# Score matmuls over 128 rows with zero-padded k pieces, and bisection on fp32 scores, in a hybrid attention layer

## Chip, core and metric

The kernel runs on one core of one Trainium2 chip. The metric is the device time of one execution in microseconds (us). Its engines are TensorE (PE in the rows; PEld is its weight load), VectorE (DVE), ScalarE (ACT), GpSimd (POOL) and SyncE (SP), which issues most DMAs.

## The reference

One encoder layer over x of 1024 frames by 1024 features, fp32. One input projection feeds three groups of heads; their outputs go through an output projection, a layer norm, a SwiGLU network of width 2816 and a second layer norm. Cut to what the change touches:

```
h = x @ w_in
# differential attention: 4 heads, two score maps each, 64 features, blocks of 128 queries
logits = einsum('bthmd,bshmd->bhmts', q, k) * scale + alibi bias, masked by chunks of 64
p = softmax(logits); attn = p[:, :, 0] - lam * p[:, :, 1]; out_b = rms_norm(attn @ v)
# sparse attention: 4 heads of 64 features; of each query's allowed keys the 256 best by an index score
score = sum over 8 index heads of w * relu(q_i @ k_i)
_, sel = lax.top_k(score, 256)
out_c = softmax(q @ k[sel] * scale + bias) @ v[sel]
```

## The kernel before

Matrix products keep fp32 accuracy by splitting an operand into a high part in fp32r (rounded) and a low part, the rest. A projection is three matmuls for each piece (`mm3`, L180 to L182): high by high, high by low, low by high.

**Scores.** A head's q and k hold 64 features for each of two score maps m. `q_stacks` puts q's high part on 64 partitions and its low part on the other 64 of one tile. `k_stacks` (L629 on) copies k's high part to both halves of `kh[m]` (a copy by ScalarE and a DMA from half to half), so that one matmul over 128 rows gives q's high plus low part by k's high part (L659, weights 128 x 128). The missing product, q's high part by k's low part, is a second matmul into the same PSUM piece (L660); k's low parts of both maps share one tile, `kl`, 64 partitions each, and the matmul works on those 64 rows alone. `softmax` does this for pieces of 256 to 512 columns, and VectorE then takes each piece out of PSUM with bias and running minimum (L664). `diff_unit` makes one block of 128 queries of a differential head (names b0 to b3), `dsa_pair` two sparse heads (c0, c1). There are 8 blocks for each of 6 pairs of maps.

**Selection.** The index scores of query blocks 2 to 7 lie in `sc_all` in fp32. The 256th largest of a row is found by bisection over the 32 bits of its key: a step counts how many scores reach a candidate. ScalarE does the counting for blocks 5 to 7, VectorE for blocks 2 to 4 (`DVE_B`; 640, 512 and 384 columns). VectorE first copies the upper 16 bits of its scores to a packed tile (`upper_halves`, L493), and counts over those for bits 31 to 16 (L497). Then `lower_halves` (L505 to L520) counts scores above the found upper half, and replaces each score by its lower 16 bits where the upper half is equal and by zero where it isn't; 16 steps more count over those (`bisect_low`, L529 to L532).

**Order.** Lists in the file say in which order attention units are made (`UNITS`), how many projection pieces go between them (`FILLS`), and how many bisection steps of either engine (`STEPS_A`, `STEPS_D`). A scheduler then interleaves the instructions at build time; each engine runs its own list in order. Tiles of 4 KB for each partition come from a ring `st` of 11 buffers: all of q, k, the packed scores, later weights. Transposed probabilities use `at`, 3 buffers. GpSimd splits weights of projections (L170, L158) and makes two small operations of each differential unit: `sn` (L692) and the power in `rsqrt` (`rs`, L198), for which VectorE waits (L704). The SwiGLU network comes after all attention, from about 650 us on.

Of the kernel before, what the change touches and what calls it, by code (L numbers as in the profile page):

```python
# [9 lines left out]
F32 = mybir.dt.float32  # L10
# [88 lines left out]
def trunk(  # L99
# [22 lines left out]
        return t if len(shape) == 2 else t.rearrange("p (a b) -> p a b", a=shape[1])  # L122

    def st(name, shape=(P, 1024), dt=F32R):
        return tl("st", 11, name, shape, dt)

    def pp(name, shape=(P, 1024), dt=F32):
        return tl("p", 5, name, shape, dt)
# [7 lines left out]
    def small(name, w=1, dt=F32, bufs=5):  # L136
        return pool.tile([P, w], dt, tag=f"s_{name}", bufs=bufs, name=name)
# [13 lines left out]
    def f(ap):  # L151
        return ap.bitcast(F32)
# [322 lines left out]
    junk, junk_a = junk2[:, 0], junk2[:, 1]  # L475
    zero = pool.tile([P, len(SEL_BLOCKS)], I32, name="zero")
    V.memset(zero, 0)
    flips, half = {}, {}

    def as_float(dst, k, e):  # L480
        t = small(f"bt_{e}", nbl[e], I32, 2)
        V.tensor_scalar(t, k, 31, 0x7FFFFFFF, op0=OP.arith_shift_right, op1=OP.bitwise_and)
        V.scalar_tensor_tensor(dst, k, -1, t, op0=OP.bitwise_xor, op1=OP.bitwise_xor)

    def upper_halves():
        free, t = 0, None
        for i in sorted(DVE_B, key=lambda i: (i == 2, -i)):
            n = P * (i + 1)
            if free < n:
                t, free = st(f"half{i}", (P, 2048), BF16), 2048  # L490
            half[i] = t[:, 2048 - free:2048 - free + n]
            free -= n
            V.tensor_copy(half[i], SC[i].bitcast(BF16)[:, 1::2])  # L493

    def count_half(th, cnt, dt):
        for j, i in enumerate(DVE_B):
            V.tensor_scalar(junk[:, 0:P * (i + 1)], half[i].bitcast(dt), th[:, j:j + 1], None,  # L497
                            op0=OP.is_ge, op1=OP.add, accum_out=cnt[:, j:j + 1])

    low = {}  # L500

    def lower_halves():
        key, nb = keys["d"], nbl["d"]
        top = small("top", nb, I32, 1)
        V.scalar_tensor_tensor(top, key, 0, flips["d"], op0=OP.bitwise_or, op1=OP.bitwise_xor)  # L505
        sg = small("sgn", nb, F32, 1)
        V.tensor_copy(sg, key)
        V.tensor_scalar(sg, sg, 0.0, None, op0=OP.is_ge)
        off = small("off", nb, F32, 1)
        V.tensor_scalar(off, sg, 65535.0, None, op0=OP.mult)  # L510
        V.tensor_scalar(sg, sg, -2.0, 1.0, op0=OP.mult, op1=OP.add)
        need = small("need_d", nb, F32, 1)
        for j, i in enumerate(DVE_B):
            n = P * (i + 1)
            t = f(top)[:, j:j + 1]
            V.tensor_scalar(junk[:, 0:n], half[i], t, None, op0=OP.is_gt, op1=OP.add, accum_out=need[:, j:j + 1])
            V.tensor_scalar(junk[:, 0:n].bitcast(U16), SC[i].bitcast(U16)[:, 0::2], sg[:, j:j + 1], off[:, j:j + 1],
                            op0=OP.mult, op1=OP.add)
            V.scalar_tensor_tensor(half[i].bitcast(U16), half[i], t, junk[:, 0:n].bitcast(U16), op0=OP.is_equal, op1=OP.mult)
        V.tensor_scalar(need, need, -1.0, TOPK - 0.25, op0=OP.mult, op1=OP.add)  # L520
        lk = small("low", nb, F32, 1)
        V.memset(lk, 0.0)
        low["need"], low["key"] = need, lk

    def bisect_low(b):
        nb, lk = nbl["d"], low["key"]
        cand = small("cand", nb, F32, 2)
        cnt = small("cnt_d", nb, F32, 2)
        V.tensor_scalar(cand, lk, float(1 << b), None, op0=OP.add)  # L529
        count_half(cand, cnt, U16)  # L530
        V.tensor_tensor(cnt, cnt, low["need"], OP.is_ge)
        V.scalar_tensor_tensor(lk, cnt, float(1 << b), lk, op0=OP.mult, op1=OP.add)  # L532
        if b == 0:
            li = small("lowi", nb, I32, 1)
            V.tensor_copy(li, lk)
            V.tensor_tensor(keys["d"], keys["d"], li, OP.bitwise_or)

    def bisect(b, e):
        if e == "d" and b == 31:
            upper_halves()  # L540
        if e == "d" and b < 16:
            if b == 15:
                lower_halves()
            bisect_low(b)
            return
        key = keys[e]
        cnt = small(f"cnt_{e}", nbl[e], F32, 2)
        fl = small(f"fl_{e}", nbl[e], I32, 2)
        if b == 31:
            cf = zero[:, 0:nbl[e]]  # L550
        else:
            cf = small(f"cf_{e}", nbl[e], I32, 2)
            V.scalar_tensor_tensor(cf, key, 1 << b, flips[e], op0=OP.bitwise_or, op1=OP.bitwise_xor)  # L553
        if e == "d":
            count_half(f(cf), cnt, BF16)
            V.tensor_scalar(fl, cnt, TOPK - 0.25, None, op0=OP.is_ge)
        else:
            for j, i in enumerate(ACT_B):
                A.activation(junk_a[:, 0:P * (i + 1)], SC[i], AF.Sign, bias=f(cf)[:, j:j + 1], accum_out=cnt[:, j:j + 1])  # L559
            V.tensor_tensor(fl, cnt, lim, OP.is_ge)  # L560
        V.scalar_tensor_tensor(key, fl, b, key, op0=OP.logical_shift_left, op1=OP.bitwise_or)
        if b == 31:
            m = pool.tile([P, nbl[e]], I32, name=f"flip_{e}")
            V.tensor_scalar(m, key, 31, 0x7FFFFFFF, op0=OP.arith_shift_right, op1=OP.bitwise_and)
            V.tensor_scalar(m, m, -1 if e == "d" else 0x7FFFFFFF, -65536 if e == "d" else -1, op0=OP.bitwise_xor, op1=OP.bitwise_and)
            flips[e] = m

    def settle():
# [60 lines left out]
    def k_stacks(col, name, rh, rl):  # L629
        wh, wl = wload(win[:, :, col:col + P], name, [P, KC, P], GP)  # L630
        yield
        kh = [st(f"{name}_h{m}") for m in range(2)]
        kl = st(f"{name}_l")
        rh += kh
        rl += [kl[0:64], kl[64:128]]
        for half in range(2):
            ps = proj_t(wh, wl, P, half)
            sl = slice(half * 512, half * 512 + 512)
            for m in range(2):
                a = slice(64 * m, 64 * m + 64)  # L640
                b = slice(64 - 64 * m, 128 - 64 * m)
                A.activation(kh[m][a, sl], ps[a], AF.Copy)
                sub(V, kl[a, sl], ps[a], f(kh[m][a, sl]))
                nc.sync.dma_start(f(kh[m][b, sl]), f(kh[m][a, sl]))
            yield

# [6 lines left out]
    def softmax(i, m, q, kh, kl, bias, slope, p):  # L653
        n = P * (i + 1)
        nm = None
        sm = small("sm")
        for o, w in pieces(n):
            ps = ps_qk("psq")
            nc.tensor.matmul(ps[:, 0:w], q[:, i * P:(i + 1) * P], kh[:, o:o + w], start=True, stop=False)  # L659
            nc.tensor.matmul(ps[:, 0:w], q[64 * m:64 * m + 64, i * P:(i + 1) * P], kl[:, o:o + w], start=False, stop=True)  # L660
            w = min(w, n - o)
            prev = BIG if nm is None else nm
            nm = small(f"nm{o}")
            V.tensor_tensor_reduce(out=p[:, o:o + w], in0=ps[:, 0:w], in1=bias[:, o:o + w], scale=-slope, scalar=prev,  # L664
                                   op0=OP.add, op1=OP.min, accum_out=nm)
        A.activation(p[:, 0:n], p[:, 0:n], AF.Exp, bias=nm, scale=-1.0, accum_out=sm)  # L666
        return p, sm

    def prio(n):
        return tc.high_priority(n)  # L670

    def attend(i, a, vsl, ps):
        nk = i + 1
        for j0 in range(0, nk, 4):
            jn = min(4, nk - j0)
            pt = ps_tr("psa")
            for j in range(jn):
                nc.tensor.transpose(pt[:, j * P:(j + 1) * P], a[:, (j0 + j) * P:(j0 + j + 1) * P], ident)
            at = tl("at", 3, "at", (P, 512))
            A.activation(at[:, 0:jn * P], pt[:, 0:jn * P], AF.Copy)  # L680
            for j in range(jn):
                nc.tensor.matmul(ps, at[:, j * P:(j + 1) * P], vsl(j0 + j), start=(j0 + j == 0), stop=(j0 + j == nk - 1))  # L682
# [96 lines left out]
    def dsa_pair(c, i):  # L779
# [10 lines left out]
        for j0 in range(0, nk, 4):  # L790
            jn = min(4, nk - j0)
            at = []
            for m in range(2):
                pt = ps_tr("psa")
                for j in range(jn):
                    nc.tensor.transpose(pt[:, j * P:(j + 1) * P], pr[m][:, (j0 + j) * P:(j0 + j + 1) * P], ident)
                at.append(tl("at", 3, "at", (P, 512)))
                copy(at[m][:, 0:jn * P], pt[:, 0:jn * P], "av"[m])
            for j in range(jn):
                for m in range(2):  # L800
                    hs = slice(64 * m, 64 * m + 64)
                    nc.tensor.matmul(ps[hs], vc[c][:, j0 + j, hs], at[m][:, j * P:(j + 1) * P],
                                     start=(j0 + j == 0), stop=(j0 + j == nk - 1))
# [171 lines left out]
            sub(V, l, r[k], f(h))  # L975
        return T

    def w4(name, tag="st", bufs=11):
        return tl(tag, bufs, name, (P, KC, P), F32R)

    def hidden(c):
# [172 lines left out]
```

## Time and profile before

| what | value |
|---|---|
| median of 3 runs | 1423.05 us (1419.74 to 1425.28) |
| the profiled execution | 1420.1 us |
| its span, first to last instruction | 1418.3 us |
| mean granted TensorE clock | 0.955 of full |
| TensorE busy | 94% of the span |
| VectorE, ScalarE, GpSimd busy | 65%, 39%, 22% |

Shares are means over stages with different limits, and a busy TensorE is one that has a matmul in its pipe, whether or not the next could have started sooner. How fast matmuls follow each other is read from the differences of their starts in the timeline.

### The profile page before, as it was taken

The page shows a single profiled execution, that of the slowest core. Times are in us where ns is not written, and L with a number is a line of the kernel's source. Part 1 is how long each engine was busy: PE and PEld are TensorE (multiplying, and loading weights), DVE is VectorE, ACT ScalarE, POOL GpSimd, SP SyncE. Part 2 cuts the span into 40 slices and gives each one's busy share as a digit, 9 for nine tenths or more (in the row PEclk, how much of TensorE's full clock was granted, in tenths as well). Part 3 has the DMA queues.
Part 4 walks back from the last instruction along what each step waited for, and adds up shares of the span by engine and source line. Part 5 has one row for each costly group of instructions (what it writes and reads, how often), then busy time and mean ns, then how long its engine had stood idle before and what let it go on. Part 6 is the DMA issues. An engine that isn't in the chain of part 4 may idle for free.

```text
span 1418.3 us, 17526 instructions
## 1 busy us (share of the span) xinstructions
PE 1329.7 (94%) x6444; PEld 1065.8 (75%) x6444; DVE 927.0 (65%) x1821; ACT 557.6 (39%) x1033; POOL 318.3 (22%) x250
## 2 busy tenths in 40 slices
PE   7568987988999999899999999999999999999997
PEld 6457665676787886557788888888888888888886
DVE  5137899797657968444859776676667655348325
ACT  4145565666785534243313322222222233213310
POOL 1203221103132144400215333233333210000003
PEclk9779998899999999889999999999999999999999
DMA  6221111101111111315402222222222248427501
GB/s 192 76 74 59 49 29 43 36 9 38 51 40 41 50 34 49 96 51 182 149 33 91 86 74 90 89 79 85 90 77 75 87 182 336 149 89 269 206 0 60
DMA packets 107685, 127.46 MB, mean 90 GB/s; under 512 B 8144, under 2 KB 80720, under 8 KB 107600
## 3 DMA queue, kind: packets, MB, share of 16 engines
q1 hardware_dynamic: 106448, 122.15, 26.4%
q10 hardware_dynamic: 1152, 4.19, 0.8%
q8 instruction: 51, 0.84, 0.3%
q14 instruction: 34, 0.28, 0.1%
HBM read 97.49 MB, written 25.69 MB: 87 GB/s over the span
## 4 chain that ended last, share of the span: by engine, by line
PE 51%; DVE 1%; DMA 0%; issue 0%; ACT 0%; DVEq 0%; ACTq 0%; SPq 0%
PE p L181 9%; PE p L182 9%; PE p L180 9%; PE psd L180 6%; PE psd L182 6%; PE psd L181 6%; PE psz L182 1%; PE psz L180 1%; PE psz L181 1%; PE pg L180 1%; PE pu L182 1%; PE pu L180 1%; PE pg L182 1%; PE pg L181 1%; PE pu L181 1%; PE pst L208 0%
## 5 line engine op out<-in xcount | busy, mean ns | idle before, releaser
L559 ACT ACTIVATE junk<-sc_all,cf_a 128x768 bf16<-128x768 f32 (+2 forms) x93 | 96.7, 1039 | 35.9 <-DVE cf_a L553 14.1
L182 PE MATMUL psn<-hi_n,xTl 128*128 128x256 f32 x320 | 99.0, 309 | 0.0
L180 PE MATMUL psn<-hi_n,xTh 128*128 128x256 f32 x320 | 97.5, 305 | 0.9 <-DVE nm L664 0.9
L181 PE MATMUL psn<-lo_n,xTh 128*128 128x256 f32 x320 | 96.8, 302 | 0.0
L666 ACT ACTIVATE pt<-pt,nm 128x128 f32<-128x128 f32 (+7 forms) x96 | 74.0, 772 | 49.4 <-DVE nm L664 47.0
L198 POOL TENSOR_TENSOR lrs<-rv,mhalf 128x1 f32<-128x1 f32 x16 | 20.6, 1286 | 307.5 <-DVE rv L195 307.5
L1017 POOL TENSOR_TENSOR s<-raw_u 128x512 f32<-128x512 f32 x20 | 27.9, 1396 | 242.4 <-DMA raw_u<-in_w_gu_dram 206.9
L180 PEld LDWEIGHTS psn<-hi_n,xTh 128*128 128x128 f32 x320 | 66.2, 207 | 4.2 <-issue 2.0
L182 PEld LDWEIGHTS psn<-hi_n,xTl 128*128 128x128 f32 x320 | 66.2, 207 | 4.2 <-issue 3.0
L181 PEld LDWEIGHTS psn<-lo_n,xTh 128*128 128x128 f32 x320 | 65.8, 206 | 3.2 <-issue 1.6
L180 PE MATMUL p<-x1Th,gh 128*128 128x512 f32 x160 | 62.2, 389 | 0.0
L181 PE MATMUL p<-x1Tl,gh 128*128 128x512 f32 x160 | 62.2, 389 | 0.0
L182 PE MATMUL p<-x1Th,gl 128*128 128x512 f32 x160 | 62.2, 389 | 0.0
L365 PE MATMUL psi<-kst,qst 128*128 128x512 f32 (+1 forms) x80 | 29.0, 398 | 32.5 <-DMA qst<-qd 21.3
L372 DVE SCALAR_TENSOR_TENSOR sc_all<-rl,iw,sc_all 128x384 f32<-128x384 f32 (+5 forms) x42 | 41.4, 1046 | 27.5 <-ACT rl L367 27.4
L1043 DVE TENSOR_TENSOR th<-p,tp 128x512 f32<-128x512 f32 x20 | 13.8, 692 | 69.1 <-DMA hd<-th 57.6
L1059 ACT ACTIVATE sg<-tp 128x512 f32<-128x512 f32 x20 | 12.7, 634 | 105.6 <-DVE tp L1058 105.6
L664 DVE CUSTOM_DVE_ANT_0 pt<-psq,dist 128x512 f32<-128x512 f32 (+3 forms) x72 | 38.8, 546 | 22.0 <-PE psq L660 21.7
L198 POOL TENSOR_TENSOR rs<-rv,mhalf 128x1 f32<-128x1 f32 x32 | 19.1, 597 | 134.5 <-DVE rv L197 79.4
L1040 ACT ACTIVATE tp<-p 128x512 f32<-128x512 f32 x20 | 12.0, 600 | 93.6 <-DVE th L1065 80.4
L367 ACT ACTIVATE rl<-psi 128x512 f32<-128x512 f32 (+1 forms) x80 | 35.4, 562 | 23.7 <-PE psi L365 21.1
L682 PEld LDWEIGHTS pso<-vb,at 128*128 128x128 f32 x288 | 39.1, 206 | 7.0 <-DVE ob L705 2.4
(679 smaller groups left out, 4168.1 us busy)
## 6 DMA issues: line engine op xcount, KB each, us to landing
raw_g<-in_w_gu_dram SPq DMA_DIRECT2D x22, 512.0 KB
raw_u<-in_w_gu_dram SPq DMA_DIRECT2D x22, 512.0 KB
hd<-th SPq DMA_DIRECT2D x22, 512.0 KB
raw_n<-in_w_in_dram SPq DMA_DIRECT2D x10, 512.0 KB
x<-in_x_dram SPq DMA_DIRECT2D x8, 512.0 KB
raw_wo<-in_w_out_dram SPq DMA_DIRECT2D x8, 512.0 KB
mx<-mixd SPq DMA_DIRECT2D x8, 512.0 KB
y<-x1d SPq DMA_DIRECT2D x8, 512.0 KB
```

Of the source, the lines that this page charges most:

```text
L180: nc.tensor.matmul(ps, lh, rh, start=first, stop=False)
L181: nc.tensor.matmul(ps, lh, rl, start=False, stop=False)
L182: nc.tensor.matmul(ps, ll, rh, start=False, stop=last)
L198: GP.tensor_tensor(o, t, mhalf[:, 0:w], OP.pow)
L365: nc.tensor.matmul(ps[:, 0:w], qst[h][:, (i - 2) * P:(i - 1) * P], kst[:, o:o + w], start=True, stop=True)
L367: A.activation(r[:, o:o + w], ps[:, 0:w], AF.Relu)
L372: V.scalar_tensor_tensor(SC[i], r[:, 0:n], wcol, SC[i], op0=OP.mult, op1=OP.add)
L559: A.activation(junk_a[:, 0:P * (i + 1)], SC[i], AF.Sign, bias=f(cf)[:, j:j + 1], accum_out=cnt[:, j:j + 1])
L664: V.tensor_tensor_reduce(out=p[:, o:o + w], in0=ps[:, 0:w], in1=bias[:, o:o + w], scale=-slope, scalar=prev, op0=OP.add, op1=OP.min, accum ...
L666: A.activation(p[:, 0:n], p[:, 0:n], AF.Exp, bias=nm, scale=-1.0, accum_out=sm)
L682: nc.tensor.matmul(ps, at[:, j * P:(j + 1) * P], vsl(j0 + j), start=(j0 + j == 0), stop=(j0 + j == nk - 1))
L1017: GP.tensor_tensor(a[:, 0:4], u[:, 0:4], u[:, 4:8], OP.add)
```

## The change

`k_stacks` takes a tile of its own for each map's low part: 64 partitions hold it, and GpSimd sets the other 64 to zero. The second score matmul takes all 128 rows of q and of that tile. Where the low part meets q's high part the product is as before, and the zero rows add nothing. The ring `st` gets a twelfth buffer. The bisection of blocks 2 to 4 counts over the fp32 scores in `sc_all` for all 32 bits; the packed tile and its two preparations go. The transposed probabilities go in turn to four parts of one fixed tile, `ats`, in place of three buffers.

```diff
     def st(name, shape=(P, 1024), dt=F32R):
-        return tl("st", 11, name, shape, dt)
+        return tl("st", 12, name, shape, dt)
...
-    def upper_halves():
...
-            V.tensor_copy(half[i], SC[i].bitcast(BF16)[:, 1::2])
-
-    def count_half(th, cnt, dt):
-        for j, i in enumerate(DVE_B):
-            V.tensor_scalar(junk[:, 0:P * (i + 1)], half[i].bitcast(dt), th[:, j:j + 1], None,
-                            op0=OP.is_ge, op1=OP.add, accum_out=cnt[:, j:j + 1])
...
-    def lower_halves():
...
-    def bisect_low(b):
...
     def bisect(b, e):
-        if e == "d" and b == 31:
-            upper_halves()
-        if e == "d" and b < 16:
-            if b == 15:
-                lower_halves()
-            bisect_low(b)
-            return
...
         if e == "d":
-            count_half(f(cf), cnt, BF16)
+            for j, i in enumerate(DVE_B):
+                V.tensor_scalar(junk[:, 0:P * (i + 1)], SC[i], f(cf)[:, j:j + 1], None,
+                                op0=OP.is_ge, op1=OP.add, accum_out=cnt[:, j:j + 1])
...
         kh = [st(f"{name}_h{m}") for m in range(2)]
-        kl = st(f"{name}_l")
+        kl = [st(f"{name}_l{m}") for m in range(2)]
         rh += kh
-        rl += [kl[0:64], kl[64:128]]
+        rl += kl
+        for m in range(2):
+            GP.memset(f(kl[m][64 - 64 * m:128 - 64 * m]), 0.0)
...
-                sub(V, kl[a, sl], ps[a], f(kh[m][a, sl]))
+                sub(V, kl[m][a, sl], ps[a], f(kh[m][a, sl]))
...
-            nc.tensor.matmul(ps[:, 0:w], q[64 * m:64 * m + 64, i * P:(i + 1) * P], kl[:, o:o + w], start=False, stop=True)
+            nc.tensor.matmul(ps[:, 0:w], q[:, i * P:(i + 1) * P], kl[:, o:o + w], start=False, stop=True)
...
+    ats = pool.tile([P, 4, 512], F32, name="ats")
+    turn = iter(range(1 << 20))
+
+    def next_at():
+        return ats[:, next(turn) % 4]
...
-            at = tl("at", 3, "at", (P, 512))
+            at = next_at()
...
-    def w4(name, tag="st", bufs=11):
+    def w4(name, tag="st", bufs=12):
```

The line numbers of the changed kernel are about 53 lower behind the removed functions: L606 and L607 are its two score matmuls, L496 its count.

TensorE, where the scores of a block of head b2 stand between pieces of the projection of b3's q (psp) and products of probabilities and values (pso); before:

```order
L682 MATMUL pso<-vb_2357,at 128x128 x3
L182 MATMUL psp<-xTh_71,lo_b3q 128x512
L659 MATMUL psq<-b2k_h_2098,b2q_1982 128x512
L180 MATMUL psp<-xTh_71,hi_b3q 128x512
L660 MATMUL psq<-b2k_l,b2q_1982 128x512
L181 MATMUL psp<-xTl_73,hi_b3q 128x512
L182 MATMUL psp<-xTh_71,lo_b3q 128x512
L659 MATMUL psq<-b2k_h_2098,b2q_1982 128x256
L682 MATMUL pso<-vb_2357,at 128x128 x4
L180 MATMUL psp<-xTh_71,hi_b3q 128x512
L660 MATMUL psq<-b2k_l,b2q_1982 128x256
L181 MATMUL psp<-xTl_73,hi_b3q 128x512
```

and now:

```order
L180 MATMUL psp<-xTh_71,hi_b3q 128x512
L181 MATMUL psp<-xTl_73,hi_b3q 128x512
L606 MATMUL psq<-b2k_h_2087,b2q_1972 128x512
L182 MATMUL psp<-xTh_71,lo_b3q 128x512
L607 MATMUL psq<-b2k_l_2089,b2q_1972 128x512
L180 MATMUL psp<-xTh_71,hi_b3q 128x512
L181 MATMUL psp<-xTl_73,hi_b3q 128x512
L606 MATMUL psq<-b2k_h_2087,b2q_1972 128x256
L182 MATMUL psp<-xTh_71,lo_b3q 128x512
L607 MATMUL psq<-b2k_l_2089,b2q_1972 128x256
L180 MATMUL psp<-xTh_71,hi_b3q 128x512
```

The two score matmuls of a piece still stand one matmul of the projection apart; what stands between them and around them has shifted by a few rows.

VectorE, where the bisection of blocks 2 to 4 (names ending in d, `half`, `junk`) passes from bit 16 to bit 15; before:

```order
L497 TENSOR_SCALAR junk_490,cnt_d<-half_1245,cf_d 128x640
L693 RECIPROCAL r_2279<-sm 128x1
L556 TENSOR_SCALAR fl_d<-cnt_d 128x3
L694 TENSOR_TENSOR r_2279<-r_2279,sn 128x1
L561 SCALAR_TENSOR_TENSOR key_d<-fl_d,key_d 128x3
L695 SCALAR_TENSOR_TENSOR pt<-pt,r_2279 128x512
L505 SCALAR_TENSOR_TENSOR top<-key_d,flip_d 128x3
L507 CAST sgn<-key_d 128x3
L516 TENSOR_SCALAR junk_490,need_d<-half_1245,top 128x384
L508 TENSOR_SCALAR sgn<-sgn 128x3
L510 TENSOR_SCALAR off<-sgn 128x3
L511 TENSOR_SCALAR sgn<-sgn 128x3
```

and now, at the same bit:

```order
L496 TENSOR_SCALAR junk_490,cnt_d<-sc_all,cf_d 128x512
L493 SCALAR_TENSOR_TENSOR cf_a<-key_a,flip_a 128x3
L496 TENSOR_SCALAR junk_490,cnt_d<-sc_all,cf_d 128x640
L498 TENSOR_SCALAR fl_d<-cnt_d 128x3
L503 SCALAR_TENSOR_TENSOR key_d<-fl_d,key_d 128x3
L493 SCALAR_TENSOR_TENSOR cf_d<-key_d,flip_d 128x3
L496 TENSOR_SCALAR junk_490,cnt_d<-sc_all,cf_d 128x384
L496 TENSOR_SCALAR junk_490,cnt_d<-sc_all,cf_d 128x512
L158 TENSOR_TENSOR b2k_l_2089<-psp,b2k_h_2087 64x512
L611 ISA pt,nm_2377<-psq,dist,nm_2372 128x256
L611 ISA nm_2377 128x1
L496 TENSOR_SCALAR junk_490,cnt_d<-sc_all,cf_d 128x640
```

Before, the preparation of the lower halves begins here; now the next count over `sc_all` follows at once.

GpSimd, after the splitting of head b2's q weights, among the small operations of the units of head b0; before:

```order
L158 TENSOR_TENSOR lo_b2q<-raw_b2q,hi_b2q 128x1024
L692 TENSOR_TENSOR sn<-sm,neglam 128x1
L198 TENSOR_TENSOR rs<-rv_1198,mhalf 128x1
L692 TENSOR_TENSOR sn<-sm,neglam 128x1
L198 TENSOR_TENSOR rs<-rv_1303,mhalf 128x1
L692 TENSOR_TENSOR sn<-sm,neglam 128x1 x2
L170 TENSOR_SCALAR hi_b2k<-raw_b2k 128x1024
L158 TENSOR_TENSOR lo_b2k<-raw_b2k,hi_b2k 128x1024
```

and now:

```order
L158 TENSOR_TENSOR lo_b2q<-raw_b2q,hi_b2q 128x1024
L645 TENSOR_TENSOR sn<-sm,neglam 128x1
L198 TENSOR_TENSOR rs<-rv_1201,mhalf 128x1
L645 TENSOR_TENSOR sn<-sm,neglam 128x1
L198 TENSOR_TENSOR rs<-rv_1301,mhalf 128x1
L645 TENSOR_TENSOR sn<-sm,neglam 128x1
L582 MEMSET b1k_l_1725 64x1024
L582 MEMSET b1k_l_1726 64x1024
L645 TENSOR_TENSOR sn<-sm,neglam 128x1
L170 TENSOR_SCALAR hi_b2k<-raw_b2k 128x1024
L158 TENSOR_TENSOR lo_b2k<-raw_b2k,hi_b2k 128x1024
```

The two memsets of head b1's low parts now stand in GpSimd's list between two `sn`. The other ten stand among its work too: b0's between two weight splits, b2's on either side of an `rs`.

## Rows read from the trace of the kernel before

**Rows 1.** The page, part 1: busy us of each engine, share of the span, instructions.
```profile
PE 1329.7 (94%) x6444; PEld 1065.8 (75%) x6444; DVE 927.0 (65%) x1821; ACT 557.6 (39%) x1033; POOL 318.3 (22%) x250
```

**Rows 2.** Source line L660: first and last of six rows, TensorE alone (144 matmuls).
```profile
L660 PE MATMUL psq<-b0k_l,b0q x24: 379/439/792, 147.7 to 185.5; 64*128 64x512 f32 x10, 64*128 64x256 f32 x8, 64*128 64x384 f32 x6
...
L660 PE MATMUL psq<-c1k_l,c1q x24: 275/498/792, 582.0 to 645.8; 64*128 64x512 f32 x10, 64*128 64x256 f32 x8, 64*128 64x384 f32 x6
```

**Rows 3.** Windows: busy us by engine in three stretches, granted clock, DMA share, GB/s.
```profile
147.00:350.00 203.00, 176.74 (x819) 131.84 (x818) 180.49 (x656) 127.56 (x296) 40.48 (x55) 0.89 0.12 32
350.00:650.00 300.00, 286.50 (x1623) 216.32 (x1621) 199.48 (x500) 159.15 (x347) 87.13 (x68) 0.93 0.18 52
650.00:1418.30 768.30, 759.97 (x3434) 626.05 (x3432) 475.40 (x558) 213.57 (x268) 166.50 (x108) 1.00 0.34 118
```

**Rows 4.** Waits from 147 to 650 us: total us, times, longest us.
```profile
DVE pt L664 <- PE psq L660: 37.6, 37, 5.8
...
PE psa L678 <- DVE pt L695: 15.0, 7, 3.9
...
DVE rs L704 <- POOL rs L198: 7.8, 14, 0.7
```

**Rows 5.** TensorE's timeline at 293 us: start us, us, instruction.
```profile
293.17 0.41 PE L182 MATMUL psn<-hi_n,xTl 128*128 128x256 f32 x1
293.38 0.38 PE L180 MATMUL psn<-hi_n,xTh 128*128 128x256 f32 x1
...
293.72 0.28 PE L182 MATMUL psn<-hi_n,xTl 128*128 128x256 f32 x1
293.84 0.28 PE L659 MATMUL psq<-b2k_h,b2q 128*128 128x256 f32 x1
294.05 0.38 PE L660 MATMUL psq<-b2k_l,b2q 64*128 64x256 f32 x1
294.36 0.38 PE L180 MATMUL psn<-hi_n,xTh 128*128 128x256 f32 x1
```

**Rows 6.** TensorE's timeline at 405 us.
```profile
405.33 0.40 PE L659 MATMUL psq<-b3k_h,b3q 128*128 128x512 f32 x1
405.56 0.28 PE L180 MATMUL psn<-hi_n,xTh 128*128 128x256 f32 x1
405.77 0.49 PE L660 MATMUL psq<-b3k_l,b3q 64*128 64x512 f32 x1
406.20 0.38 PE L181 MATMUL psn<-lo_n,xTh 128*128 128x256 f32 x1
```

**Rows 7.** Windows of source line L660 alone: TensorE and its weight load.
```profile
147.00:350.00 203.00, 30.02 (x63) 12.35 (x63) 0.89 0.12 32
```

**Rows 8.** Groups by form on VectorE, 147 to 460 us: busy us, mean ns, idle before.
```profile
L497 DVE TENSOR_SCALAR_CACHE_REDUCE junk<-half,cf_d 128x640 bf16<-128x640 bf16 x15 | 13.1, 877 | 0.2
...
L531 DVE TENSOR_TENSOR cnt_d<-cnt_d,need_d 128x3 f32<-128x3 f32 x16 | 5.6, 351 | 0.2
...
L556 DVE TENSOR_SCALAR fl_d<-cnt_d 128x3 int32<-128x3 f32 x16 | 3.7, 229 | 0.2
...
L606 DVE TENSOR_SCALAR_CACHE_REDUCE eq<-sc_all,thr_d 128x640 f32<-128x640 f32 x1 | 0.9, 872 | 0.0
```

**Rows 9.** Source lines L493, L516, L517, L519: duration ns min/median/max, starts.
```profile
L493 DVE COPY half<-sc_all x3: 360/411/475, 146.2 to 147.7; 128x640 bf16<-128x640 bf16 x1, 128x512 bf16<-128x512 bf16 x1, 128x384 bf16<-128x384 bf16 x1
...
L516 DVE TENSOR_SCALAR_CACHE_REDUCE junk<-half,top x3: 612/748/879, 244.9 to 249.4; 128x384 bf16<-128x384 bf16 x1, 128x512 bf16<-128x512 bf16 x1, 128x640 bf16<-128x640 bf16 x1
...
L517 DVE TENSOR_SCALAR junk<-sc_all,sgn,off x3: 479/547/600, 246.1 to 251.3; 128x384 uint16<-128x384 uint16 x1, 128x512 uint16<-128x512 uint16 x1, 128x640 uint16<-128x640 uint16 x1
...
L519 DVE SCALAR_TENSOR_TENSOR half<-half,top,junk x3: 621/752/877, 246.6 to 254.9; 128x384 uint16<-128x384 bf16 x1, 128x512 uint16<-128x512 bf16 x1, 128x640 uint16<-128x640 bf16 x1
```

**Rows 10.** Groups by form on GpSimd, whole span.
```profile
masks.py:197 POOL MEMSET ident<- 128x128 f32 x1 | 0.2, 204 | 0.3 <-POOLq L1141 0.3
```

**Rows 11.** GpSimd's timeline at 139 us, with the wait before.
```profile
138.63 1.06 POOL L170 TENSOR_SCALAR hi_b1k<-raw_b1k 128x1024 fp32r<-128x1024 f32 x1 [7.52 <-PE psp L181]
```

More of the change, by code (lines that the diff above doesn't have):

```diff
@@ L477, in trunk @@
     V.memset(zero, 0)
-    flips, half = {}, {}
+    flips = {}
     def as_float(dst, k, e):
@@ L483, in as_float @@
         V.scalar_tensor_tensor(dst, k, -1, t, op0=OP.bitwise_xor, op1=OP.bitwise_xor)
-    def upper_halves():
[L486 to L492, printed above, removed]
-            V.tensor_copy(half[i], SC[i].bitcast(BF16)[:, 1::2])
-    def count_half(th, cnt, dt):
-        for j, i in enumerate(DVE_B):
-            V.tensor_scalar(junk[:, 0:P * (i + 1)], half[i].bitcast(dt), th[:, j:j + 1], None,
-                            op0=OP.is_ge, op1=OP.add, accum_out=cnt[:, j:j + 1])
@@ L500, in trunk @@
-    low = {}
-    def lower_halves():
[L503 to L523, printed above, removed]
@@ L525, in bisect_low @@
-    def bisect_low(b):
[L526 to L536, printed above, removed]
@@ L564, in bisect @@
             V.tensor_scalar(m, key, 31, 0x7FFFFFFF, op0=OP.arith_shift_right, op1=OP.bitwise_and)
-            V.tensor_scalar(m, m, -1 if e == "d" else 0x7FFFFFFF, -65536 if e == "d" else -1, op0=OP.bitwise_xor, op1=OP.bitwise_and)
+            if e == "a":
+                V.tensor_scalar(m, m, 0x7FFFFFFF, None, op0=OP.bitwise_xor)
+            else:
+                V.tensor_scalar(m, m, -1, None, op0=OP.bitwise_xor)
             flips[e] = m
@@ L796, in dsa_pair @@
                     nc.tensor.transpose(pt[:, j * P:(j + 1) * P], pr[m][:, (j0 + j) * P:(j0 + j + 1) * P], ident)
-                at.append(tl("at", 3, "at", (P, 512)))
+                at.append(next_at())
                 copy(at[m][:, 0:jn * P], pt[:, 0:jn * P], "av"[m])
```

## Prediction

> **What bounds the kernel now.** I read the busy shares first: TensorE 94%, VectorE 65%, the others far below [rows 1]. A share is a mean over stages, so I then cut the span into windows at the first and the last of the second score matmuls, about 147 and 650 us [rows 2]. Behind 650 us TensorE is busy 760.0 of 768.3 us at full granted clock [rows 3]; no edit removes work there, so whatever is won ahead of 650 us should reach the end, as that stage merely starts sooner. All the rest is decided in the two windows before it. From 350 to 650 us TensorE is busy 286.5 of 300 us and VectorE 199.5: TensorE sets the pace. From 147 to 350 us TensorE is busy 176.7 of 203 us and VectorE 180.5: both are near their limit and take turns. In the table of waits [rows 4] the reader should see both directions: VectorE waited 37.6 us for the second score matmul, and TensorE's transposes waited 15.0 us for VectorE's probabilities. So in these windows time saved on either engine may count, and the question is how much of it.
>
> **The second score matmul.** The busy column hides its cost, so I take differences of starts. At 293 us an ordinary 256-column matmul over 128 rows is followed after 0.12 us (293.72 to 293.84). The same matmul ahead of the 64-row one takes 0.21 (293.84 to 294.05), and the 64-row one is followed after 0.31 (294.05 to 294.36) [rows 5]. Against 0.12 each that is 0.09 + 0.19 = 0.28 us lost around one matmul. At 405 us the ordinary 512-column step is 0.23 (405.33 to 405.56); the step into the 64-row matmul is 0.21 where 256 columns want 0.12, and the step out of it 0.43 where 512 want 0.23: 0.29 us [rows 6]. The zero-padded matmul has the shape of its neighbours, so I take their steps for it. The rows name 144 of them, 24 for each of six heads [rows 2]: 144 x 0.29 = 41.8 us of TensorE's time. By place, 63 lie from 147 to 350 us [rows 7], worth 18.3 us, and the other 81 behind it, worth 23.5 us. None of this shows as idle, since a 64-row matmul is recorded as 439 to 498 ns long in the medians [rows 2] and overlaps the next.
>
> From 350 to 650 us the bound is the whole 23.5 us below, and nothing above, where each step ended in front of another wait. TensorE isn't alone there, because transposes wait for probabilities and heads of the sparse part go through three engines in turn; I take three quarters, 17.6 us.
>
> **The bisection on VectorE.** A count over 640 packed 16-bit scores takes 877 ns; the same operation over 640 fp32 scores in the final selection takes 872 [rows 8]. So the 96 counts cost the same in both forms, and what goes is preparation. The three copies take 0.36, 0.41 and 0.48 us; the counts above, the low pieces and the masks take 2.24, 1.63 and 2.25 [rows 9]: together 7.4 us. Some nine operations on 128 x 3 numbers go with them, priced by the 229 ns of such an operation [rows 8] at no more than 2.1 us; I take 1.5. Each of the 16 lower steps compares by an operation of 351 ns where the upper steps compare by one of 229: 16 x 0.12 = 2.0 us. The sum is 10.9 us less on VectorE, all from 147 to 350 us and shortly behind.
>
> The Trainium skill, VectorE: DVE Perf Modes, section "The perf-mode tier table", says that a scalar operation on 16-bit data in SBUF runs at four elements a cycle and on fp32 at two. By its figures for 2048 elements (693 and 1227 ns) the fp32 counts would cost an estimated 0.26 ns an element more, 1536 x 32 x 0.26 = 12.8 us, and VectorE would gain nothing. The measured counts show no difference between the two types, so the measurement decides.
>
> **The window from 147 to 350 us.** If VectorE sets the pace throughout, the gain there is its 10.9 us; if TensorE does, it is 18.3. They alternate, and I take the middle, 14.6 us. The lower bound of the gain is nothing, when the waits of one for the other merely move.
>
> **GpSimd's memsets.** Twelve, 64 x 1024. The nearest row below is a memset of 128 x 128, 0.20 us [rows 10]; above, a weight split of 128 x 1024, 1.06 [rows 11]. I take 1.0, since the elements for each partition are those of the split: 12 us in all on an engine busy 22% [rows 1]. For head b0 the cover is a wait of 7.52 us just behind the split of b1's q [rows 11], and two memsets fit in. The others stand between `sn` and `rs`, and behind them VectorE waits already, 7.8 us in 14 times [rows 4]. If every pair of the other five held one up by its 2 us, that would be 10 us; they fall where GpSimd is idle four times out of five, so I take 1 us.
>
> **The rest.** The twelfth buffer replaces the one that packed scores held, while two heads at a time take one more each; a wait for it would be TensorE's or ScalarE's at a head's start. No row prices that beside the memsets' waits; I bound it by nothing and by their 10 us, and take nothing. The fourth buffer for transposed probabilities can only take away a wait, and costs nothing. The SwiGLU stage has one buffer more and TensorE never waits there long enough to notice: 8.3 us idle in 768 [rows 3].
>
> **Sum.** 17.6 + 14.6 - 1 = 31.2 us. From the profiled 1420.1 us that is 1388.9; the median of the three runs is 3 us above that execution, so I predict 1392 us.
>
> **The rivals.**
>
> *Half is absorbed.* VectorE keeps the pace up to 350 us and the chains between engines keep it behind, so that only VectorE's 10.9 us and a quarter of the 23.5 arrive: 17 us, and 11 with some of the memsets' 10. For it speaks VectorE's 180.5 of 203 us; against it, that VectorE itself waits 37.6 us for this matmul [rows 4]. 1406 us, from 1400 to 1412.
>
> *More than the steps.* The granted clock averages 0.89 and 0.93 in the two windows [rows 3]. A mean of two levels, 1.0 and 0.5, makes that (0.11 x 203 + 0.07 x 300) x 2 = 87 us at 1.2 GHz. There a 256-column step takes 0.21 us (293.17 to 293.38) against 0.12 [rows 5]. If TensorE, with fewer stalls, kept 2.4 GHz in a third of that, 29 x 0.43 = 12 us come on top, and with all 41.8 us of steps the time is 1371. For it speaks that in the last window, where TensorE never pauses, the clock is 1.00; against it, that TensorE still waits for VectorE.
>
> *The fp32 counts are slower after all*, by the 12.8 us above (the output is 16-bit, which the fp32 row isn't): then the first window gives at most a few us, and the time is about 1404. The two equal rows speak against it.
>
> *No change.* The steps only exposed waits that ended at the same time anyway, and the VectorE savings were idle already: 1416 to 1430 us. The 37.6 us of VectorE's waits for this very matmul speak against it.
>
> *Slower.* One mechanism: a memset in GpSimd's list waits for a buffer of the ring that TensorE still reads, and `sn` or `rs` of earlier units stand behind it, for which VectorE and then the transposes wait. It needs more than 31 + 7 = 38 us over the five later pairs, 7.6 us each, to bring the time above 1430. For it speaks that memsets now stand in the middle of that list; against it, that ScalarE's copies into `kh` already take buffers of this ring at the same place, and that the longest waits of TensorE and VectorE are for results [rows 4].
>
> **Chances and range.** The forecast 0.50 (its own range 1384 to 1400), half absorbed 0.16, more than the steps 0.15, slower counts 0.02, no change 0.09, slower 0.08. Half a per cent, 7 us, is about what a measurement of this kernel can tell from no change. Faster is 0.83, the same 0.09, slower 0.08. The range that leaves out the last two, and holds the others with their bounds, is 1371 to 1412.
>
> **What would show it.** TensorE's steps into and out of the second score matmul at 0.12 and 0.23 us; the count over `sc_all` at about 877 ns; no waits behind GpSimd's memsets; the last score matmul some 30 us earlier than 645.8 and the stage behind it as long as before; a higher mean clock from 147 to 650 us if the third case holds. I am wrong if the steps shrink and the last score matmul doesn't move, or if the stage behind 650 us grows.

## Result and profile after

The changed kernel takes 1373.7 us (median of 4 runs, 1372.2 to 1378.0) against 1422.5 us for the kernel before beside it: a ratio of 0.966 (95% interval [0.963, 0.969]), 48.8 us less. That is inside the range, but 18 us below the predicted 1392 and outside the forecast's own 1384 to 1400; it comes to lie beside the rival "more than the steps" (1371). The profiled execution took 1374.4 us, with a span of 1372.5 us.

The page of the changed kernel, part 1, answers to [rows 1]; VectorE's busy time is 17.4 us less, TensorE's 64.6 us.

```profile
PE 1265.1 (92%) x6444; PEld 1052.3 (77%) x6444; DVE 909.6 (66%) x1797; ACT 554.2 (40%) x1033; POOL 328.5 (24%) x262
```

Windows of the changed kernel, with the columns of [rows 3], cut 768.3 us ahead of the span's end:

```profile
147.00:604.20 457.20, 400.81 (x2443) 337.17 (x2444) 360.77 (x1122) 284.75 (x644) 134.26 (x134) 0.94 0.18 52
604.20:1372.50 768.30, 759.51 (x3427) 625.64 (x3427) 476.20 (x557) 212.95 (x268) 167.10 (x107) 1.00 0.34 116
```

The last 768.3 us are as before: TensorE busy 759.5 us at full clock, for 760.0 [rows 3]. The stage ahead of them holds the same number of matmuls as before and is 457.2 us long where it was 503.0, so all 45.8 us of the span were won there.

TensorE's timeline of the changed kernel at 354 us, where scores (L606, L607) stand between matmuls of a projection:

```profile
354.47 0.28 PE L606 MATMUL psq<-b3k_h,b3q 128*128 128x256 f32 x1
354.59 0.28 PE L181 MATMUL psn<-lo_n,xTh 128*128 128x256 f32 x1
354.71 0.28 PE L607 MATMUL psq<-b3k_l,b3q 128*128 128x256 f32 x1
354.83 0.28 PE L182 MATMUL psn<-hi_n,xTl 128*128 128x256 f32 x1
```

Every start follows the one before by 0.12 us. The 0.21 and 0.31 around L660 [rows 5] are gone. Among matmuls of 512 columns, at 402 us, every step is 0.23:

```profile
401.91 0.39 PE L182 MATMUL psp<-xTh,lo_c0q 128*128 128x512 f32 x1
402.14 0.40 PE L607 MATMUL psq<-b3k_l,b3q 128*128 128x512 f32 x1
402.37 0.39 PE L180 MATMUL psp<-xTh,hi_c0q 128*128 128x512 f32 x1
```

The count over 640 scores (groups by form on VectorE), now over fp32 data:

```profile
L496 DVE TENSOR_SCALAR_CACHE_REDUCE junk<-sc_all,cf_d 128x640 bf16<-128x640 f32 x31 | 27.2, 876 | 0.5
```

876 ns against 877 over packed 16-bit scores [rows 8].

Waits of the changed kernel from 147 to 604.2 us, to be read beside [rows 4]:

```profile
DVE pt L611 <- PE psq L607: 17.0, 17, 5.6
...
PE psa L631 <- DVE pt L648: 13.2, 12, 2.4
...
DVE rs L657 <- POOL rs L198: 9.5, 15, 2.5
```

VectorE waits half as long for the second score matmul (17.0 for 37.6 us). No wait stands behind the memsets, each about 0.95 us; the source line of the first two:

```profile
L582 POOL MEMSET b0k_l<- x2: 947/948/949, 130.0 to 131.0; 64x1024 f32 x2
```

### The profile page after: what moved, and what is told of

It is laid out like the page before. It is cut to its first block, busy times and chain, and to the rows that moved or that the text cites. A ratio compares the mean times of both kernels' runs of the same rounds, so it can differ in the third digit from the quotient of the medians.

```text
span 1372.5 us, 17547 instructions
## 1 busy us (share of the span) xinstructions
PE 1265.1 (92%) x6444; PEld 1052.3 (77%) x6444; DVE 909.6 (66%) x1797; ACT 554.2 (40%) x1033; POOL 328.5 (24%) x262
## 4 chain that ended last, share of the span: by engine, by line
PE 51%; DVE 1%; issue 1%; DMA 0%; POOL 0%; ACT 0%; DVEq 0%; SPq 0%; POOLq 0%; ACTq 0%
PE p L182 9%; PE p L181 9%; PE p L180 9%; PE psd L180 6%; PE psd L181 6%; PE psd L182 6%; PE psz L180 1%; PE psz L182 1%; PE psz L181 1%; PE pu L182 0%; PE pu L180 0%; PE pu L181 0%; PE pg L182 0%; PE pg L180 0%; PE pg L181 0%
## 5 line engine op out<-in xcount | busy, mean ns | idle before, releaser
L180 PE MATMUL psn<-hi_n,xTh 128*128 128x256 f32 x320 | 94.6, 296 | 0.0
L182 PE MATMUL psn<-hi_n,xTl 128*128 128x256 f32 x320 | 94.0, 294 | 0.0
L496 DVE TENSOR_SCALAR_CACHE_REDUCE junk<-sc_all,cf_d 128x384 bf16<-128x384 f32 (+2 forms) x93 | 69.1, 743 | 1.8
L635 PE MATMUL pso<-vb,ats 128*128 128x128 f32 x288 | 40.6, 288 | 10.0 <-DVE ob L658 3.7
L635 PEld LDWEIGHTS pso<-vb,ats 128*128 128x128 f32 x288 | 38.5, 202 | 13.6 <-DVE ob L658 4.6
L631 PE MATMUL psa<-ident,pt 128*128 128x128 f32 x144 | 26.2, 300 | 23.9 <-DVE pt L648 13.2
```

The source lines that it names most:

```text
L180: nc.tensor.matmul(ps, lh, rh, start=first, stop=False)
L182: nc.tensor.matmul(ps, ll, rh, start=False, stop=last)
L496: V.tensor_scalar(junk[:, 0:P * (i + 1)], SC[i], f(cf)[:, j:j + 1], None, op0=OP.is_ge, op1=OP.add, accum_out=cnt[:, j:j + 1])
```

## Experiments

The theories: (A) the 64-row matmuls cost their 0.29 us of steps each, and nearly all of it reaches the end; (B) VectorE's relief, or the buffers that the bisection gives back, is a large part of the gain; (C) part of it is the granted clock, or an order of instructions that the scheduler happened to give. Ratios are to the kernel before, run beside each; kernels that didn't run side by side are compared by their ratios. The times of e3, e4, e5 and e7 lie in none of the ranges that were expected for them.

Two cuts serve for all of them: the last second score matmul of head b2 (half of the 144 are done) and the last one of c1, both from that matmul's source line. In the changed kernel:

```profile
L607 PE MATMUL psq<-b2k_l,b2q x24: 281/389/545, 273.6 to 343.4; 128*128 128x512 f32 x10, 128*128 128x256 f32 x8, 128*128 128x384 f32 x6
...
L607 PE MATMUL psq<-c1k_l,c1q x24: 274/392/628, 545.7 to 593.5; 128*128 128x512 f32 x10, 128*128 128x256 f32 x8, 128*128 128x384 f32 x6
```

In the kernel before they stand at 374.4 and 645.8 us. The table calls the first stretch the time from 147 us to b2's cut, the second that from b2's to c1's; PE busy and clock are those of the second. Medians rest on 4 to 11 executions, stretches on one each, and executions of one kernel differ: those of the kernel before took 1414 to 1430 us, at a mean granted clock of 0.948 to 0.963.

| kernel | 2nd score matmul | bisection over | median us | ratio [95%] | 1st stretch | 2nd stretch | PE busy | clock |
|---|---|---|---|---|---|---|---|---|
| before | 64 rows | 16-bit | 1422.5 | 1 | 227.4 | 271.4 | 258.5 | 0.92 |
| e10 | 64 | 16-bit | 1424.3 | 1.002 [0.999, 1.005] | 236.0 | 271.0 | 259.4 | 0.92 |
| e4 | 64 | fp32 | 1425.4 | 1.004 [1.001, 1.006] | 226.8 | 278.4 | 262.2 | 0.91 |
| e1 | 64 | fp32 | 1412.6 | 0.995 [0.992, 0.997] | 208.7 | 270.8 | 258.7 | 0.91 |
| e7 | 64, in pairs | fp32 | 1403.7 | 0.991 [0.989, 0.993] | 211.0 | 265.4 | 245.0 | 0.92 |
| e8 | 128, in pairs | fp32 | 1392.2 | 0.982 [0.980, 0.984] | 209.7 | 257.3 | 232.1 | 0.94 |
| e2 | 128 | 16-bit | 1393.1 | 0.981 [0.978, 0.984] | 212.2 | 249.9 | 223.9 | 0.97 |
| e3 | 128 | 16-bit | 1390.5 | 0.979 [0.976, 0.982] | 222.5 | 249.4 | 229.2 | 0.95 |
| changed | 128 | fp32 | 1373.7 | 0.966 [0.963, 0.969] | 196.4 | 250.1 | 226.0 | 0.95 |
| e9 | 128 | fp32 | 1382.3 | 0.972 [0.968, 0.976] | 207.6 | 248.4 | 223.7 | 0.95 |
| e11 | 128 | fp32 | 1379.0 | 0.970 [0.966, 0.974] | 202.0 | 252.6 | 226.9 | 0.95 |
| e5 | 128 | fp32 | 1378.6 | 0.973 [0.971, 0.975] | 200.8 | 254.7 | 232.1 | 0.95 |
| e12 | 128 | fp32 | 1381.7 | 0.971 [0.968, 0.975] | 207.4 | 247.7 | 224.4 | 0.98 |
| e6 | 128 | fp32 | 1388.4 | 0.980 [0.978, 0.983] | 206.7 | 253.9 | 223.1 | 0.95 |

**e1: the matmul back on 64 rows, all else as changed.**

```diff
-        rl += kl
+        rl += [kl[0][0:64], kl[1][64:128]]
...
-            nc.tensor.matmul(ps[:, 0:w], q[:, i * P:(i + 1) * P], kl[:, o:o + w], start=False, stop=True)
+            nc.tensor.matmul(ps[:, 0:w], q[64 * m:64 * m + 64, i * P:(i + 1) * P], kl[:, o:o + w], start=False, stop=True)
```

> The changed kernel with one edit undone: the second score matmul works on 64 rows again (memsets, tiles, ring of 12, fp32 bisection and the fixed tile for transposed probabilities stay). Steps theory (the gain is the 0.29 us of TensorE around each 64-row matmul, 41.8 us, and some clock): 1412 to 1422 us, and the steps of 0.21 and 0.31 us around a 256-column one are back. Rival (VectorE's relief, the buffers or the new order gave most of it): 1390 us or less.

1412.6 us. Each engine's list holds the same instructions in the same order as in the changed kernel, so nothing but the row count differs. The rows are worth (0.9946 - 0.9662) x 1422.5 = 40 us by the ratios, 33.7 us by the two profiled spans (1406.2 and 1372.5). TensorE's timeline of e1:

```profile
405.99 0.39 PE L606 MATMUL psq<-b3k_h,b3q 128*128 128x512 f32 x1
406.22 0.39 PE L181 MATMUL psp<-xTl,hi_c0q 128*128 128x512 f32 x1
406.54 0.49 PE L607 MATMUL psq<-b3k_l,b3q 64*128 64x512 f32 x1
406.96 0.50 PE L182 MATMUL psp<-xTh,lo_c0q 128*128 128x512 f32 x1
```

A 512-column step takes 0.23 (405.99 to 406.22); into L607 it takes 0.32, out of it 0.42: 0.28 us, as in [rows 6]. Theory A holds for the larger part of the gain. What it turns into is read from the second stretch; windows of e1, and then of the changed kernel:

```profile
355.70:626.50 270.80, 258.66 (x1487) 196.96 (x1486) 176.64 (x455) 142.88 (x313) 79.97 (x66) 0.91 0.18 50
```

```profile
343.40:593.50 250.10, 225.98 (x1488) 189.00 (x1487) 177.27 (x454) 143.15 (x316) 81.51 (x67) 0.95 0.19 55
```

TensorE's busy time falls by 32.7 us, and the stretch by 20.7; its idle time grows from 12.1 to 24.1. The steps of 72 matmuls explain 72 x 0.29 = 20.9 of the 32.7. The clock explains about 10: at 0.91 and 0.95 the stretch had (0.09 x 270.8 - 0.05 x 250.1) x 2 = 23.7 us more and fewer at 1.2 GHz, and a us there is worth 0.43, by the steps of [rows 5]. So in this stretch the 64 rows cost twice, by their steps and by a lower clock, and about a third of the relief ended in front of other waits. (The clock has two digits; the 10 us are good to some 2.)

The first stretch of e1 is another case:

```profile
147.00:355.70 208.70, 186.75 (x914) 138.29 (x912) 184.78 (x663) 140.50 (x326) 52.13 (x68) 0.96 0.15 38
```

The changed kernel took 196.4 us there, with TensorE busy 164.6. So TensorE's busy time fell by 22.2 us and the stretch by 12.3, though the clock was on the side of e1: 0.96 against 0.93, by the same working 10.8 us fewer at 1.2 GHz, worth 4.6. Over both stretches of these two executions the clock then explains some 6 of the 33.7 us. Whole executions show a larger difference of the clock: 0.950 to 0.961 in the six of e1, 0.966 to 0.974 in the four of the changed kernel. The profiled execution of e1 has the highest clock and the shortest time of its six.

**e2: the changed kernel with the bisection of before**, its packed scores in a tile of their own. **e3: the kernel before with the zero rows alone** (own tiles for the low parts, memsets, ring of 12, the packed scores in a tile of their own). **e4: the kernel before with the fp32 bisection alone.** Their edits are parts of the change's diff; the lines of e2 and e3 that it doesn't have are in `upper_halves`:

```diff
-        free, t = 0, None
+        t, free = pool.tile([P, 1536], BF16, name="halves"), 0
...
+            half[i] = t[:, free:free + n]
+            free += n
```

> The changed kernel with the bisection of blocks 2 to 4 on 16-bit pieces put back (the pieces in a tile of their own, 128-row matmuls kept). Steps theory: VectorE's 10.9 us are mostly hidden now that TensorE paces, 1374 to 1385 us. Rival (VectorE set the pace up to 350 us, and its relief is a large part): 1388 us or more.

> The kernel before with the zero-padded 128-row matmul alone (two low tiles, memsets, ring of 12; 16-bit bisection in a tile of its own, three buffers of transposed probabilities). Steps theory: 1374 to 1386 us, that is 37 to 49 us of the 49 by this edit alone. Rival (the parts share the gain): 1395 to 1410 us.

> The kernel before with the fp32 bisection alone (64-row matmuls, ring of 11, three buffers kept). Steps theory: VectorE has 11 to 19 us less to do, of which TensorE hides most: 1412 to 1422 us. Rival (VectorE's relief counts in full): 1403 to 1411 us.

The zero rows alone give 2.1% (30 us), the bisection alone loses 0.35% (5 us), and the two with the buffers give 3.4%. In the second stretch there is no riddle: e2 and e3 need 249.9 and 249.4 us, as the changed kernel does, e4 278.4. The first stretch is where parts don't add up: 222.5 with the zero rows, 226.8 with the bisection, 196.4 with both, from 227.4; and e1, with all but the rows, has 208.7. Windows of e3 there, and then of the changed kernel:

```profile
147.00:369.50 222.50, 176.49 (x945) 149.16 (x944) 200.26 (x702) 145.22 (x336) 51.71 (x69) 0.90 0.14 38
```

```profile
147.00:343.40 196.40, 164.59 (x906) 140.67 (x907) 177.94 (x656) 138.68 (x323) 51.07 (x67) 0.93 0.14 38
```

In e3 VectorE is busy 200.3 of 222.5 us and TensorE 176.5: relieved of the steps, TensorE idles 46 us behind a VectorE that is the pace. Its transposes wait for the probabilities for 16.9 us in e3 and 23.9 in e2 (15.0 before); the row of e2 in its table of waits, 147 to 620.7 us:

```profile
PE psa L684 <- DVE pt L701: 23.9, 14, 5.8
```

In e4 it is the other way round: VectorE's relief meets a TensorE busy 204.0 of 226.8 us. So theory B in its plain form (VectorE's relief is worth its 10 us by itself) is wrong: it is worth nothing while the 64-row steps stand, and about 1.5% (e2 against the changed kernel, 21 us) once they are gone. How much of those 21 us is order is the question of e9, and e5 gives a second value.

**e5: three pool buffers for transposed probabilities** in place of the four parts of a fixed tile. **e6: each memset four times**, 36 more.

```diff
-            at = next_at()
+            at = tl("at", 3, "at", (P, 512))
...
```

```diff
-            GP.memset(f(kl[m][64 - 64 * m:128 - 64 * m]), 0.0)
+            for _ in range(4):
+                GP.memset(f(kl[m][64 - 64 * m:128 - 64 * m]), 0.0)
```

> The changed kernel with transposed probabilities back in three buffers given out by the scheduler. If the fourth buffer only takes away a wait that hardly occurs: 1371 to 1378 us. If it is a part of the gain that I priced at nothing (the 64-row kernels with and without it stand 13 us apart): 1382 to 1390 us.

> The changed kernel with each memset made four times, 36 more of 0.95 us on GpSimd. If they are hidden, as I took them: 1371 to 1378 us. If VectorE waits behind them for the small operations in GpSimd's list: up to 34 us more, 1385 or above.

e5 is 0.7% slower than the changed kernel, by ratios, e6 1.4%. Against e3, e5 has the fp32 bisection and nothing else: (0.9788 - 0.9731) x 1422.5 = 8 us, where e2 and the changed kernel gave 21. With 128 rows the bisection is then worth 8 to 21 us, by pairs that differ in their order too. Read alone, e6 would price a memset at (0.9801 - 0.9662) x 1422.5 / 36 = 0.55 us, and the twelve of the change at 7 us. But both kernels come out of the scheduler in another order than the changed one, so the next two ask what another order costs by itself.

**e9: 36 memsets of one column each in the changed kernel; e10: the same in the kernel before.**

```diff
             GP.memset(f(kl[m][64 - 64 * m:128 - 64 * m]), 0.0)
+            for _ in range(3):
+                GP.memset(f(kl[m][64 - 64 * m:128 - 64 * m, 0:1]), 0.0)
```

> The changed kernel with 36 more memsets of one column each (in place of the 36 whole ones of the run with four memsets): the same instructions more in GpSimd's list, with next to no work. If that run's loss of 14 to 20 us was GpSimd's time: 1371 to 1378 us here. If it was the new order that the scheduler made around them: a shift of 7 us or more in either direction again.

> The kernel before with 36 memsets of one column into the low tile ahead of its subtractions: no change in the work, another draw of the scheduler's order. If the order is worth little: within 5 us of the kernel before. If orders differ by as much as the fp32 bisection alone lost (5 us) or as the four memsets did: 5 to 15 us away, in either direction.

Source line of e9's small memsets, first of six rows:

```profile
L584 POOL MEMSET b0k_l<- x6: 92/94/94, 134.2 to 135.0; 64x1 f32 x6
```

They are 36 x 0.094 = 3.4 us of GpSimd's time, nobody waits for them, and e9 is slower than the changed kernel by 0.6% (0.9717 to 0.9662, 8 us; the intervals overlap a little; the spans differ by 9.3). The whole loss lies in the first stretch, 207.6 for 196.4 us, while the second is even 1.7 us shorter. In the kernel before the same addition gives no difference (1.002 [0.999, 1.005]), though its first stretch in the one profiled execution is 236.0 for 227.4 us, at a clock of 0.88 for 0.90. So some 10 us of the first stretch of the changed kernel most likely belong to the order it happened to get (8 by the medians), and e6, which loses as much there (206.7), can't be read as GpSimd's time. Between e6 and e9 lie 12 us by the ratios and 4 by the spans; were all of it the 36 longer memsets, the twelve of the change would cost 1 to 4 us. That is an estimate and no bound, since the two kernels differ in their order too.

**e11: four fixed tiles for the low parts, zeroed once at the start** (4 memsets in place of 12, and the low parts no longer take turns in the ring). **e12: a ring of 11 buffers.**

```diff
+    kls = [[pool.tile([P, S], F32R, name=f"kl{a_}{m}") for m in range(2)] for a_ in range(2)]
...
-        kl = [st(f"{name}_l{m}") for m in range(2)]
+        kl = kls[next(kturn) % 2]
...
```

```diff
-        return tl("st", 12, name, shape, dt)
+        return tl("st", 11, name, shape, dt)
...
```

> The changed kernel with four fixed tiles for the low parts, by turns for the heads, whose zero halves are set once at the start: 4 memsets instead of 12, all far ahead of the attention, the ring of 12 kept beside them. If memsets among the units cost what the run with four says (about 5 us for twelve): 1364 to 1371 us. If they are hidden: 1371 to 1377 us. If the order decides: anywhere within 10 us of 1374.

> The changed kernel with the ring of 11 buffers, the one part not undone so far; its order stays close to that of the changed kernel. If the twelfth buffer only replaces what the low parts take: a head's projection waits for a buffer now and then, 1374 to 1384 us. If the ring is a large part of the gain: 1390 us or more.

Neither is faster: 0.970 and 0.971 against 0.966. Memsets that are gone bring nothing that can be seen, and e12's 0.5% is all that the twelfth buffer shows. Both losses are of e9's size and mostly in the first stretch (202.0 and 207.4), so they can't be told from order. No kernel that was run beats the changed one.

**e7 and e8: is it 64 rows, or the change between 64 and 128?** In e7, on the changed kernel, the scores of both maps are made together, both first matmuls and then both second ones, on 64 rows in opposite halves; e8 is the same with 128 rows. Both have one order of instructions.

```diff
-            nc.tensor.matmul(ps[:, 0:w], q[:, i * P:(i + 1) * P], kh[:, o:o + w], start=True, stop=False)
-            nc.tensor.matmul(ps[:, 0:w], q[:, i * P:(i + 1) * P], kl[:, o:o + w], start=False, stop=True)
+            for m in range(2):
+                hi = nc.tensor.matmul(ps[m][:, 0:w], q[m][:, i * P:(i + 1) * P], kh[m][:, o:o + w], start=True, stop=False).ins
+            with tc.issue_after(hi):
+                for m in range(2):
+                    nc.tensor.matmul(ps[m][:, 0:w], q[m][64 * m:64 * m + 64, i * P:(i + 1) * P], kl[m][:, o:o + w], start=False, stop=True)
...
```

> 64 rows as in the kernel before, on the changed kernel's tiles, but the second matmuls of both maps of a piece are made one behind the other, behind both first ones. If the loss is at the change from 128 to 64 rows and back, it is paid for once in a pair and the two matmuls on different rows run side by side: about half of the 41.8 us and more comes back, 1375 to 1395 us. If 64-row matmuls are slow in themselves, the time stays at that of the 64-row version, 1410 us or more.

> The changed kernel (128 rows) in the paired order, as the control of the run before. The order of the two maps alone should matter little: 1368 to 1385 us. If the paired order holds three PSUM buffers longer and lets TensorE wait: 1390 or more.

TensorE's timeline of e7:

```profile
157.79 0.50 PE L610 MATMUL psq<-b0k_l,b0q 64*128 64x512 f32 x2
158.23 0.58 PE L182 MATMUL psp<-xTh,lo_b1q 128*128 128x512 f32 x1
```

The first row is two 64-row matmuls of 512 columns. Together they are 0.50 us long, as a single one is (0.49 [rows 6]), and they are followed after 0.44 us, where a single one took 0.43: on opposite halves they ran side by side, and the second of a pair is next to free, against 0.23 for a 128-row one. The difference of e7 and e8 is then (0.9908 - 0.9823) x 1422.5 = 12 us, where unpaired it was 40 (e1 against the changed kernel). Not all are paired: in e7's timeline 50 pairs stand together, and the other 44 of the 144 still stand alone among 128-row matmuls; at 0.29 us each these are 12.8 us, about the whole difference. That fits a price on each passage between row shapes, paid once for a pair, but e7 doesn't part it from the time that running side by side saves. For the passage speak the steps: a lone one loses 0.28 us at 256 columns and 0.29 at 512 [rows 5, rows 6], so the loss doesn't grow with the work. The pairing itself loses: e8 is 1.6% slower than the changed kernel, and why stays open.

## Why the prediction was right, and where it was too small

**What bounds the kernel.** Right: the last 768.3 us hold the same work in every kernel, with TensorE busy 757 to 760 us at a clock of 1.00, and all of the gain lies between 147 us and their start.

**The steps.** Right in size and place: 0.12 and 0.23 us now, and e1 brings the 0.28 us back. The Trainium skill, TensorEngine Tiling (Array Packing), section "Key Properties", says that a change of the tiling mode drains the engine; e7 fits it, since the second of two neighbours on 64 rows is next to free. The page gives no price; the timelines give 0.28 to 0.29 us for a lone 64-row matmul among 128-row ones.

**The three quarters behind 350 us** (17.6 us). Too small. The sum's cut at 350 us lies behind the 63rd second score matmul, which starts at 349.2 us before and at 320.2 now: from there to c1's cut 23.3 us were won, of a full 23.5, and 29.0 ahead of it, where the sum had 14.6. In the stretches of the table: the second has 72 of the 144 and gained 271.4 - 250.1 = 21.3 us, about the full worth of its steps, 20.9. Not that nothing was absorbed: TensorE's work fell by 32.7 us (e1 against the changed kernel) and a third of that became idle time. What the sum lacked was the clock, which the rival "more than the steps" had: about 10 us in this stretch by e1, and 8 by the kernel before (0.92 to 0.95).

**The middle in the window from 147 to 350 us** (14.6 us). This is the step that failed most: the first stretch gained 31.0 us, where the middle for its 72 matmuls would be 15.9. The sum took the gains of the two engines as alternatives, because the engines alternate. In fact either alone brought little and both together much: 4.9 us with the zero rows alone, 0.6 with the bisection alone, 31.0 together. About 11 of the 31 are luck, a favourable order (e9), which no reading of the profile before could have given. The runs don't take the other 20 apart. The clock rose from 0.90 to 0.93, worth 7.7 us by the working of e1, which the sum didn't have. The rows by themselves, with the order kept, gave 12.3 us (e1), and e1 without them was already 18.7 us shorter than the kernel before, at a clock of 0.96. That the 20 us are the full 72 x 0.29 = 20.9 us of the stretch's steps is therefore not shown.

**The parts add up:** 31.0 + 21.3 to c1's cut, less 6.5 between that cut and the stage behind (4.2 us before, 10.7 now), is the span's 45.8.

**The bisection on VectorE.** The counts cost the same in both types, as [rows 8] had it, and the rival of slower counts is out. The Trainium skill, VectorE: DVE Perf Modes, section "The perf-mode tier table", would have made the 16-bit ones faster; 877 and 876 ns for 640 elements disagree with it for this operation, which also sums its output. VectorE's busy time in the stage fell by 380.0 - 360.8 = 19.2 us with the whole change, by 8 in e4 (372.0), where 10.9 were predicted. Busy time can't settle which is right: with the same VectorE instructions it differs as much between two orders, 927.0 us before and 919.1 in e10, 909.6 in the changed kernel and 919.8 in e9, over the whole span.

**GpSimd's memsets, and buffers.** Each memset took 0.95 us, where 1.0 was taken, and no wait stands behind them. Costs of a few us aren't excluded, as e6, e11 and e12 can't be told from order.

**The rivals.** "Half is absorbed" is out, and so is "no change". "Slower" is out: no memset waits. "More than the steps" gave the right time (its own terms, 41.8 and 12 off 1423, make 1369), and its mechanism is half of the reason: the mean clock of the stage went from 0.92 to 0.94, worth some 11 us by the working of e1. The 41.8 us of steps and the clock's part together came as a net gain of some 40 (e1), the rest ending in waits. That the time came to lie there is in part luck: with another order and the same work it is 1382 us (e9), just beside the forecast's own range.

What stays open: how much of e1's own 0.5% is the bisection, the ring, the fixed tile, or order; of what the first stretch's 20 us consist; and why a lower clock goes with 64 rows.

## What to carry to other kernels

Read the cost of a matmul from the differences of starts around it and its neighbours: that showed 0.29 us for a lone 64-row matmul, which no idle time shows. Where two engines take turns, relief of one may be worth little and relief of both more than the sum (here the zero rows alone won 30 us and the bisection alone lost 5, and both won 38 in e5 and 49 in the changed kernel), so price such edits together. Before reading a loss of half a per cent as the cost of an added operation, add as many operations of no size: here that alone cost 8 us.

## What was not expected of the hardware

The granted clock went with the row shape. In the second stretch it was 0.91 to 0.92 in all five kernels with 64-row matmuls, and 0.94 to 0.98 in the nine with 128 rows; with the same order of instructions it was 0.91 against 0.95 (e1, changed) and 0.92 against 0.94 (e7, e8). Over whole executions it was 0.950 to 0.961 in e1 and 0.966 to 0.974 in the changed kernel, 0.957 to 0.959 in e7 and 0.960 to 0.966 in e8. In the first stretch there is no such rule: e1 had 0.96 there, the changed kernel 0.93.

Two 64-row matmuls on opposite halves ran side by side: a pair of 512 columns took 0.50 us together (e7).
